# Five moving operands stored packed, each row at 192 bytes modulo 512

## The chip, the cores and the metric

The kernel runs on one core of one Trainium2 chip. The metric is the device time of one execution in microseconds (us). The kernel before takes 1623.28 us, the median of three runs (1623.12 to 1624.36). A difference of 0.2% (3.2 us) is about what a measurement of this kernel can tell from none.

## What is computed

The reference is one layer of a decoder over 272 tokens (16 meta tokens and 256 real ones) with 2048 channels: a mixer of two branches (forgetting attention and gated linear attention) and an MLP with a squared ReLU. Cut to the parts that matter here:

```python
proj = xn @ w_in                                   # 2048 -> 13336, all branches' inputs
o_fox = forgetting_attention(fq, fk, fv, ff, b_forget)
o_gla = head_rmsnorm(gated_linear_attention(gq, gk, gv, g_log)) * silu(gr)
y = sigmoid(gate_fox) * (o_fox @ w_o_fox) + sigmoid(gate_gla) * (o_gla @ w_o_gla)
h = h + y @ w_out
h = h + square(relu(rmsnorm(h) @ w1)) @ w2         # 2048 -> 8192 -> 2048
return rmsnorm(h)[:, 16:]
```

All inputs and weights are float32, and some 290 MB of weights are read once.

## The kernel before, in words

Channels lie on the 128 partitions and tokens on the free axis. A product takes one block of 128 output columns of a weight matrix: 16 row tiles (KT = 16) of 128 by 128 weights against the 16 row tiles of an activation, summed in one PSUM bank.

float32 accuracy comes from splitting each factor in two float32r parts. `next_weights` (L125) takes the next block off the list that `stream` (L40) lays out, as two halves of 8 row tiles: SP issues the load of `raw` (L118), ACT rounds it to `whi` (L120), DVE makes the rest `wlo` (L121). The pool holds five halves of each, so loads and splits run ahead of the products until a buffer is missing. The activation is split the same way by `split_to` (L168) or by a pair like L793 and L794, into an upper and a lower part that lie in one tile.

`gemm2` (L139) is the product that the change touches. For each of its row tiles it calls `mac2` (L135), which issues two matmuls: `whi` times upper and lower part at once, 512 columns wide (L136), and `wlo` times the upper part, 256 columns (L137). Each matmul is preceded by a load of its 128 columns of weights into the array (LDWEIGHTS). This text calls the two matmuls of one row tile, the wide and the narrow one, **a pair**. So 16 pairs make a product of 2048 inputs, and 8 pairs one of the forgetting branch's outputs, which have 1024.

The moving operands of `gemm2`, in the order of their use:

| operand | what it is | pairs | row step, bytes | lower part behind the upper, bytes | first row modulo 512 | row starts modulo 512 |
|---|---|---|---|---|---|---|
| `x` (L231) | normalised input | 928 | 2176 | 1088 | 128 | 128, 256, 384, 0 in turn |
| `of` (L633) | output of forgetting attention | 128 | 2048 | 1024 | 128 | all at 128 |
| `og` (L434) | output of linear attention | 256 | 2112 | 1056 | 64 | 64, 128, 192, ... in turn |
| `y` (L752) | gated sum | 256 | 2176 | 1024 | 128 | 128, 256, 384, 0 in turn |
| `x2` (L760) | input of the MLP | 1024 | 2112 | 1024 | 64 | 64, 128, 192, ... in turn |
| `a` (L822, four tiles) | hidden layer, a quarter each | 960 | 2176 | 1088 | 64 | 64, 192, 320, 448 in turn |

Where the lower part is 1024 bytes behind the upper one, the 512 columns of L136 are one unbroken run; else they are two runs with a gap between. The addresses are those of the built program. The rows of weights are 512 bytes each, and all of them start at 128 modulo 512. `a` is also read by the products of the last four output blocks, outside `gemm2`: narrow ones at L848, and L864 with 128 columns of each part.

`operand` (L221) makes the tiles of `og`, `y`, `x2` and `a`, with a step per row and an offset; `of` is a plain tile. Tiles with the tag "s1" (`x`, `y`, `a`) share one place, and so do those with the tag "s2" (`room`, `og`, `x2`, `whi_last`), as wide as its widest tile, 33,792 bytes a partition. `room` is scratch of the first half of the kernel.

Order of the work: four heads of linear attention and eight of forgetting attention, all on `x`; then 8 rounds of two output blocks, with gate products on `x`, then `of`, then `og`; then 16 products on `y`; then four times 16 products on `x2` and 16 on `a`. Within an engine a scheduler orders the instructions at build time.

Of the kernel before, what the change touches and what calls it, by code (L numbers as in the profile page):

```python
# [7 lines left out]
F32 = mybir.dt.float32  # L8
F32R = mybir.dt.float32r
# [7 lines left out]
P = 128  # L17
D = 2048
KT = D // P
NM = 16  # L20
NT = 256
NA = NM + NT
EPS = 1e-6
FOX_H, FOX_D = 8, 128
# [41 lines left out]
def trunk(ctx: ExitStack, tc: tile.TileContext, hT, w_small, w_all, consts, w_alpha2, out):  # L66
# [3 lines left out]
    def nm(s):  # L70
        serial[0] += 1
        return f"{s}_{serial[0]}"

    const = ctx.enter_context(tc.tile_pool(name="const", bufs=1))
    keep = ctx.enter_context(tc.tile_pool(name="keep", bufs=1))
# [49 lines left out]
    def next_weights(keep_hi=None):  # L125
        c = chunk[0]
        chunk[0] += 1
        parts = []
        for i in range(2):
            hi, lo, step = weight_half(c, i, None if keep_hi is None else keep_hi[:, HK * i : HK * (i + 1), :])  # L130
            step(0, HK)
            parts.append((hi, lo))
        return lambda k: (parts[k // HK][0][:, k % HK, :], parts[k // HK][1][:, k % HK, :])
# [5 lines left out]
    def gemm2(w, x, k0=0, nk=KT):  # L139

        ps = bank(pg, "ps")
        for k in range(nk):
            hi, lo = w(k0 + k)
            mac2(ps, hi, lo, x[:, k], k == 0, k == nk - 1)
        issued()
        return ps
# [12 lines left out]
    def total(ps, t=None):  # L159

        b = tmp.tile([P, NT], F32, tag="evb", name=nm("evb"))
        nc.scalar.copy(b, ps[:, NT:512])  # L162
        if t is None:
            t = tmp.tile([P, NT], F32, tag="evt", name=nm("evt"), bufs=4)
        nc.vector.tensor_tensor(t, ps[:, 0:NT], b, op=ALU.add)  # L165
        return t
# [51 lines left out]
            done = t + P  # L218
        nc.tensor.matmul(ps[:, 0:n], ones[:, 0:P], d, start=True, stop=True)

    def operand(pool, name, per_k, per_half, at=0, tag=None):  # L221


        kw = {} if tag is None else {"tag": tag}
        t = pool.tile([P, KT, per_k], F32R, name=nm(name), **kw)
        return t[:, :, at : at + per_half + NT].rearrange("p k (o t) -> p k o t", t=NT) if per_half == NT else \
            t[:, :, at : at + 2 * per_half].rearrange("p k (o t) -> p k o t", t=per_half)[:, :, :, 0:NT]


    h = keep.tile([P, KT, NA + 3], F32, name="h")  # L230
# [2 lines left out]
    ident, scan = cons[:, 0:P], cons[:, P : P + NA]  # L233
    ggn, ba, bf = cons[:, 400:416], cons[:, 416:424], cons[:, 424:425]

    room = keep.tile([P, KT * 2 * NT], F32, tag="s2", name="room")
    at_room = [0]

    def take(*shape):
# [13 lines left out]
    def gain(i, k):  # L253
        return h[:, k, NA + i : NA + i + 1]
# [57 lines left out]
    for s in range(KT // 2):  # L312
# [5 lines left out]
        for kk in range(2):  # L318
            k = 2 * s + kk
# [8 lines left out]
        at = [(w[0][:, c], w[1][:, c]) for w, n in ((wa, 4), (wb, 3)) for c in range(n)]  # L328
# [101 lines left out]
    og_box = []  # L430

    def og_tile():
        if not og_box:
            og_box.append(operand(keep, "og", 528, 264, tag="s2"))  # L434
        return og_box[0]

    def gla_gates(ts):
# [20 lines left out]
    def gla_head(hd, sg, ready=None):  # L458
# [122 lines left out]
        def scale():  # L581
            pr = st["pr"]
            spread(pr, st["y"], (0, P), NT)
            nc.scalar.copy(rg, pr[:, 0:NT])
            for i in range(4):
                j = 4 * hd + i
                nc.vector.scalar_tensor_tensor(oT[:, i, :], oT[:, i, :], ggn[:, j : j + 1], rg, op0=ALU.mult,
                                               op1=ALU.mult)
                nc.vector.tensor_tensor(oT[:, i, :], oT[:, i, :], st["sg"][:, i, :], op=ALU.mult)
                split_to(og_tile()[:, j, 0, :], og_tile()[:, j, 1, :], oT[:, i, :])  # L590
# [34 lines left out]
    for hd in range(1, GLA_H):  # L625
        gla_head(hd, None)
    flush()
    og = og_tile()


    cum.close()
    late = ctx.enter_context(tc.tile_pool(name="late", bufs=1, reuse_waits="tile"))
    of = late.tile([P, FOX_H, 2, NT], F32R, name="of")  # L633
    negc = late.tile([P, FOX_H, NA], F32, name="negc")
    nc.gpsimd.dma_start(negc.rearrange("p h t -> p (h t)"), fdram.to_broadcast([P, FOX_H * NA]))
    fox = ExitStack()
# [105 lines left out]
    for j0 in range(0, KT, 2):  # L742
        gates = ahead if j0 == 0 else [gate() for _ in range(4)]
        w = next_weights()
        for j in range(2):
            t = total(gemm2(w, of, k0=8 * j, nk=8))
            nc.vector.tensor_tensor(gates[2 * j], gates[2 * j], t, op=ALU.mult)
        for j in range(2):
            t = total(gemm2(next_weights(), og))
            nc.vector.tensor_tensor(t, gates[2 * j + 1], t, op=ALU.mult)  # L750
            nc.vector.tensor_tensor(yf[:, j0 + j, :], gates[2 * j], t, op=ALU.add)
    y = operand(keep, "y", 544, NT, at=16, tag="s1")  # L752
    for j in range(KT):
        split_to(y[:, j, 0, :], y[:, j, 1, :], yf[:, j, :])
    mix.close()
# [1 line left out]


    ht = h[:, :, NM:NA]
    x2 = operand(keep, "x2", 528, NT, tag="s2")  # L760

    def square_sum(j, acc):
        if j == 0:
            nc.scalar.activation(acc, ht[:, j, :], AF.Square)
        else:
            sq = gat.tile([P, NT], F32, tag="hsq", name=nm("hsq"))
            nc.scalar.activation(sq, ht[:, j, :], AF.Square)  # L767
            nc.gpsimd.tensor_tensor(acc, acc, sq, op=ALU.add)  # L768

    def add_residual(j, ps):  # L770
        b = tmp.tile([P, NT], F32, tag="evb", name=nm("evb"))
        nc.scalar.copy(b, ps[:, NT:512])
        nc.vector.tensor_tensor(ht[:, j, :], ps[:, 0:NT], ht[:, j, :], op=ALU.add)
        nc.vector.tensor_tensor(ht[:, j, :], ht[:, j, :], b, op=ALU.add)
# [38 lines left out]
    def relu2(a, f, ps):  # L813
        t = total(ps)
        nc.vector.scalar_tensor_tensor(t, t, 0.0, r2b, op0=ALU.max, op1=ALU.mult)
        s = gat.tile([P, NT], F32, tag="asq", name=nm("asq"))
        nc.vector.tensor_tensor(s, t, t, op=ALU.mult)
        split_to(a[:, f, 0, :], a[:, f, 1, :], s)

    acc = gat.tile([P, NT], F32, tag="acc", name="acc3", bufs=1)  # L820
    for g in range(NG):
        a = operand(keep, "a", 544, 272, tag="s1")  # L822
        held = []
        for f in range(KT):
            ps = gemm2(next_weights(), x2)
            if g == 0 and f == 0:
                held.append(ps)
                continue
            if g == 0 and f == 1:
                relu2(a, 0, held.pop())  # L830
            relu2(a, f, ps)
        last = g == NG - 1
        for j in range(KT - NL if last else KT):
            add_residual(j, gemm2(next_weights(), a))
            if last:
                square_sum(j, acc)
                nc.scalar.activation(ht[:, j, :], ht[:, j, :], AF.Identity, scale=gain(2, j))
                if j == 0:
                    tc.keep_in_program_order(nc.scalar.preload_act_table_set("sqrt_and_others"))
# [55 lines left out]
    v, p, none = nc.vector, nc.gpsimd, lambda: None  # L895
# [81 lines left out]
```

## Time and profile before

| | us |
|---|---|
| median of three runs | 1623.28 |
| the profiled execution | 1623.76 |
| its span, first to last instruction | 1621.7 |
| TensorE busy with matmuls (PE) | 1609.0 |
| weight loads (PEld) | 1447.0 |
| VectorE (DVE) | 1030.6 |
| ScalarE (ACT) | 787.8 |
| GpSimd (POOL) | 92.8 |

A row of the profile's groups names the line of the kernel, the engine, the operation, the tiles written and read, shapes and a count, then the busy time and the mean duration of one in ns, then the idle time before. Buffer numbers are left out of tile names, so that `x2` shows as `x`; the two are told apart by time, since `x` is last read at 786 us and `x2` first at 892 us. Matmuls overlap in the pipeline: the end of one, and so its duration, is modelled and reaches past the next one's start. The time that a matmul costs is the distance from its start to the next start. The view in order of time gives starts to 0.01 us.

### The profile page before, as it was taken

How to read it: one execution, taken by the hardware profiler on the slowest of the kernel's cores; microseconds unless marked ns; L12 is line 12 of the kernel's file. 1: busy time of each engine (PE TensorE's matmuls, PEld its weight loads, DVE VectorE, ACT ScalarE, POOL GpSimd, SP SyncE). 2: the span in 40 equal slices, each digit the busy share in tenths (PEclk: the TensorE clock that was granted, in tenths of full speed). 3: DMA queues.
4: the chain of work that ended last, by engine and by line, in shares of the span. 5: the costliest groups of instructions: out<-in, count | busy, mean ns of one | idle time of the engine just before them, and what ended most of it. 6: DMA issues, size and time to landing. Idle time of an engine off the chain costs nothing.

```text
span 1621.7 us, 25628 instructions
## 1 busy us (share of the span) xinstructions
PE 1609.0 (99%) x10000; PEld 1447.0 (89%) x10000; DVE 1030.6 (64%) x1589; ACT 787.8 (49%) x1212; POOL 92.8 (6%) x144
## 2 busy tenths in 40 slices
PE   9999999999999999999999999999999999999997
PEld 8999999999998888888888888888888888888887
DVE  7866747476555555555677766567655676567654
ACT  6655444454445444444555444444444444444553
POOL 1000000010000000000011000000000000000022
PEclk9999999999999999999999999999999999999998
DMA  9444445454445555555555555555565555555552
GB/s 315 149 142 159 163 158 170 155 197 158 156 157 174 189 186 191 185 191 185 190 188 192 183 189 188 190 187 189 181 195 188 190 187 189 188 189 188 187 180 89
DMA packets 90841, 292.96 MB, mean 181 GB/s; under 512 B 9160, under 2 KB 21712, under 8 KB 90592
## 3 DMA queue, kind: packets, MB, share of 16 engines
q1 hardware_dynamic: 89472, 289.69, 55.1%
q8 instruction: 78, 1.28, 0.3%
q0 software_dynamic: 176, 1.12, 0.2%
q10 hardware_dynamic: 1072, 0.52, 0.1%
q14 instruction: 43, 0.35, 0.1%
HBM read 289.19 MB, written 2.11 MB: 180 GB/s over the span
## 4 chain that ended last, share of the span: by engine, by line
PE 99%; DMA 0%; ACT 0%; DVE 0%; SPq 0%; issue 0%; DVEq 0%; ACTq 0%
PE ps L136 51%; PE ps L137 26%; PE psa L155 5%; PE psa L154 5%; PE psa L153 5%; PE ps L334 1%; PE ps L864 1%; PE ps L339 1%; PE pa L504 1%; PE ps L848 0%; DMA h<-hT_dram 0%; PE po L568 0%; PE pz L402 0%; PE po L569 0%; PE pq L665 0%; PE po L182 0%
## 5 line engine op out<-in xcount | busy, mean ns | idle before, releaser
L121 DVE TENSOR_TENSOR wlo<-raw,whi 128x1024 fp32r<-128x1024 f32 x522 | 639.7, 1225 | 497.4 <-ACT whi L120 496.1
L120 ACT CAST whi<-raw 128x1024 fp32r<-128x1024 f32 x522 | 548.3, 1050 | 744.1 <-PE ps L136 502.0
L136 PE MATMUL ps<-x,whi 128*128 128x512 f32 x1952 | 685.8, 394 | 0.0
L137 PE MATMUL ps<-x,wlo 128*128 128x256 f32 x1952 | 548.0, 281 | 0.0
L136 PEld LDWEIGHTS ps<-x,whi 128*128 128x128 f32 x1952 | 366.4, 188 | 83.2
L137 PEld LDWEIGHTS ps<-x,wlo 128*128 128x128 f32 x1952 | 367.1, 188 | 0.0
L136 PE MATMUL ps<-a,whi 128*128 128x512 f32 x960 | 335.8, 394 | 0.0
L137 PE MATMUL ps<-a,wlo 128*128 128x256 f32 x960 | 269.7, 282 | 0.0
L136 PEld LDWEIGHTS ps<-a,whi 128*128 128x128 f32 x960 | 180.1, 188 | 41.0
L153 PE MATMUL psa<-x,whi 128*128 128x272 f32 x640 | 186.3, 291 | 0.0
L155 PE MATMUL psa<-x,whi 128*128 128x272 f32 x640 | 186.0, 291 | 0.0
L154 PE MATMUL psa<-x,wlo 128*128 128x272 f32 x640 | 184.5, 288 | 0.0
L137 PEld LDWEIGHTS ps<-a,wlo 128*128 128x128 f32 x960 | 181.4, 189 | 0.4
L153 PEld LDWEIGHTS psa<-x,whi 128*128 128x128 f32 x640 | 121.1, 189 | 0.7
L154 PEld LDWEIGHTS psa<-x,wlo 128*128 128x128 f32 x640 | 120.4, 188 | 0.2
L155 PEld LDWEIGHTS psa<-x,whi 128*128 128x128 f32 x640 | 120.2, 188 | 0.1
L136 PE MATMUL ps<-og,whi 128*128 128x512 f32 x256 | 89.9, 393 | 0.0
L136 PE MATMUL ps<-y,whi 128*128 128x512 f32 x256 | 89.1, 392 | 0.0
L768 POOL TENSOR_TENSOR acc<-acc,hsq 128x256 f32<-128x256 f32 x26 | 28.8, 1110 | 774.4 <-ACT hsq L767 774.4
L137 PE MATMUL ps<-y,wlo 128*128 128x256 f32 x256 | 71.8, 281 | 0.0
L137 PE MATMUL ps<-og,wlo 128*128 128x256 f32 x256 | 71.7, 280 | 0.0
L165 DVE TENSOR_TENSOR evt<-ps,evb 128x256 f32<-128x256 f32 x158 | 65.8, 417 | 0.2 <-ACT evb L162 0.2
(263 smaller groups left out, 1384.7 us busy)
## 6 DMA issues: line engine op xcount, KB each, us to landing
raw<-w_all_dram SPq DMA_DIRECT2D x537, 512.0 KB, 4.0
raw<-w_all_dram SPq DMA_DIRECT2D x7, 384.0 KB, 6.0
h<-hT_dram SPq DMA_DIRECT2D x7, 275.0 KB, 6.1
out_dram<-h SPq DMA_DIRECT2D x5, 256.0 KB, 2.6
negc<-fdram POOLq DMA_DIRECT2D x1, 1088.0 KB, 6.1
raw<-w_all_dram SPq DMA_DIRECT2D x2, 256.0 KB, 3.7
raw<-w_all_dram SPq DMA_DIRECT2D x2, 192.0 KB, 3.8
room<-w_small_dram SPq DMA_DIRECT2D x1, 320.0 KB, 6.9
```

The lines of the kernel that those rows point to most:

```text
L120: nc.scalar.copy(hi[:, k, :], r)
L121: nc.vector.tensor_tensor(lo[:, k, :], r, hi[:, k, :].bitcast(F32), op=ALU.subtract)
L136: nc.tensor.matmul(ps, hi, x, start=first, stop=False)
L137: nc.tensor.matmul(ps[:, 0:NT], lo, x[:, 0, :], start=False, stop=last)
L153: nc.tensor.matmul(ps[:, 0:n], hi, x[:, k, 0, :], start=(k == 0), stop=False)
L154: nc.tensor.matmul(ps[:, 0:n], lo, x[:, k, 0, :], start=False, stop=False)
L155: nc.tensor.matmul(ps[:, 0:n], hi, x[:, k, 1, :], start=False, stop=(k == KT - 1))
L165: nc.vector.tensor_tensor(t, ps[:, 0:NT], b, op=ALU.add)
L334: nc.tensor.matmul(ps, hi, x[:, k, :, NM:NA], start=st, stop=False)
L339: nc.tensor.matmul(ps[:, 0:NT], lo, x[:, k, 0, NM:NA], start=False, stop=sp)
L504: nc.tensor.matmul(dst, k[:, a, :], q[:, a, :], start=(a == 0), stop=(a == 1))
L768: nc.gpsimd.tensor_tensor(acc, acc, sq, op=ALU.add)
```

## The change

`operand` makes all five tiles `of`, `og`, `y`, `x2` and `a`. Rows are 2048 bytes, upper and lower part side by side, and `at` floats ahead of the first row place it: 32 floats (128 bytes) in the tiles that start at 64 modulo 512, and 16 floats (64 bytes) in `of`, whose tile starts at 128. So each row of the five starts at 192 modulo 512. `room` is made as wide as `og` was, which keeps the place of "s2" at 33,792 bytes and the tiles of weights where they were, at 128 modulo 512. `x` is as before. The tiles of the pool of `of` that lie behind it move by 64 bytes.

```diff
-    def operand(pool, name, per_k, per_half, at=0, tag=None):
-        kw = {} if tag is None else {"tag": tag}
-        t = pool.tile([P, KT, per_k], F32R, name=nm(name), **kw)
-        return t[:, :, at : at + per_half + NT].rearrange("p k (o t) -> p k o t", t=NT) if per_half == NT else \
-            t[:, :, at : at + 2 * per_half].rearrange("p k (o t) -> p k o t", t=per_half)[:, :, :, 0:NT]
+    def operand(pool, name, at, nk=KT, **kw):
+        t = pool.tile([P, at + nk * 2 * NT], F32R, name=nm(name), **kw)
+        return t[:, at:].rearrange("p (k o t) -> p k o t", o=2, t=NT)
...
-    room = keep.tile([P, KT * 2 * NT], F32, tag="s2", name="room")
+    room = keep.tile([P, 264 * 2 * KT], F32, tag="s2", name="room")
...
-            og_box.append(operand(keep, "og", 528, 264, tag="s2"))
+            og_box.append(operand(keep, "og", 32, tag="s2"))
...
-    of = late.tile([P, FOX_H, 2, NT], F32R, name="of")
+    of = operand(late, "of", 16, FOX_H)
...
-    y = operand(keep, "y", 544, NT, at=16, tag="s1")
+    y = operand(keep, "y", 32, tag="s1")
...
-    x2 = operand(keep, "x2", 528, NT, tag="s2")
+    x2 = operand(keep, "x2", 32, tag="s2")
...
-        a = operand(keep, "a", 544, 272, tag="s1")
+        a = operand(keep, "a", 32, tag="s1")
```

In the built programs the instructions of every engine stand in the same order and number; on all of them only one wait differs, a copy on GpSimd (L655) that no longer waits for DVE.

## The prediction, as put on record before the run

> **What bounds the kernel now.** I read the page's busy times first, then the chain that ended last, then the clock.
>
> ```profile
> PE 1609.0 (99%) x10000; PEld 1447.0 (89%) x10000; DVE 1030.6 (64%) x1589; ACT 787.8 (49%) x1212; POOL 92.8 (6%) x144
> ```
> ```profile
> PE 99%; DMA 0%; ACT 0%; DVE 0%; SPq 0%; issue 0%; DVEq 0%; ACTq 0%
> PE ps L136 51%; PE ps L137 26%; PE psa L155 5%; PE psa L154 5%; PE psa L153 5%; PE ps L334 1%; PE ps L864 1%; PE ps L339 1%; PE pa L504 1%; PE ps L848 0%; DMA h<-hT_dram 0%; PE po L568 0%; PE pz L402 0%; PE po L569 0%; PE pq L665 0%; PE po L182 0%
> ```
> ```profile
> core 0: 1621.7 us, clock 0.997
> ```
>
> TensorE sets the end from first to last: 99% of the chain, and L136 with L137, the pairs of `gemm2`, are 77% of it. The granted clock is 0.997, so there is no throttle to win back. A nanosecond per pair counts one to one, as long as nothing else takes over. How many pairs there are, from the groups (`x` holds 928 pairs of `x` itself and 1024 of `x2`):
>
> ```profile
> L136 PE MATMUL ps<-x,whi 128*128 128x512 f32 x1952 | 685.8, 394 | 0.0
> ...
> L136 PE MATMUL ps<-a,whi 128*128 128x512 f32 x960 | 335.8, 394 | 0.0
> ...
> L136 PE MATMUL ps<-og,whi 128*128 128x512 f32 x256 | 89.9, 393 | 0.0
> L136 PE MATMUL ps<-y,whi 128*128 128x512 f32 x256 | 89.1, 392 | 0.0
> ```
>
> With 128 pairs of `of` (below), 960 + 1024 + 256 + 256 + 128 = 2624 pairs read an operand that the change moves. What a pair costs I take from the view in order of time, from the first wide matmul of a stage to the first of the next:
>
> ```profile
> 511.50 0.39 PE L136 MATMUL ps<-of,whi 128*128 128x512 f32 x1
> ...
> 517.15 0.40 PE L136 MATMUL ps<-og,whi 128*128 128x512 f32 x1
> ...
> 528.35 0.39 PE L136 MATMUL ps<-x,whi 128*128 128x512 f32 x1
> ...
> 802.94 0.39 PE L136 MATMUL ps<-y,whi 128*128 128x512 f32 x1
> ...
> 892.11 0.39 PE L136 MATMUL ps<-x,whi 128*128 128x512 f32 x1
> ...
> 1071.93 0.40 PE L136 MATMUL ps<-x,whi 128*128 128x512 f32 x1
> ...
> 1161.31 0.39 PE L136 MATMUL ps<-a,whi 128*128 128x512 f32 x1
> ...
> 1250.90 0.40 PE L136 MATMUL ps<-x,whi 128*128 128x512 f32 x1
> ```
>
> - `of`: 16 pairs in 517.15 - 511.50 = 5.65 us, 353.1 ns each
> - `og`: 32 pairs in 528.35 - 517.15 = 11.20 us, 350.0 ns
> - `y`: 256 pairs in 892.11 - 802.94 = 89.17 us, 348.3 ns
> - `x2`: 256 pairs in 1161.31 - 1071.93 = 89.38 us, 349.1 ns
> - `a`: 256 pairs in 1250.90 - 1161.31 = 89.59 us, 350.0 ns
>
> All pairs together: 960 x 350.0 + 1024 x 349.1 + 256 x 348.3 + 256 x 350.0 + 128 x 353.1 ns = 336.0 + 357.5 + 89.2 + 89.6 + 45.2 = 917.5 us, a mean of 349.6 ns. The same work differs by 5 ns a pair with the layout alone. Inside one product of `x2` the spread is larger; these are wide matmuls of four rows in turn (starts at 64, 128, 192 and 256 modulo 512):
>
> ```profile
> 1099.86 0.39 PE L136 MATMUL ps<-x,whi 128*128 128x512 f32 x1
> ...
> 1100.21 0.40 PE L136 MATMUL ps<-x,whi 128*128 128x512 f32 x1
> ...
> 1100.57 0.39 PE L136 MATMUL ps<-x,whi 128*128 128x512 f32 x1
> ...
> 1100.91 0.40 PE L136 MATMUL ps<-x,whi 128*128 128x512 f32 x1
> ```
>
> The row is found by counting: 1100.57 lies 28.64 us behind 1071.93, which is 5 products of 5.586 us and 2.03 pairs, so it is the third row. The row at 128 takes 0.36 us to the next pair, that at 192 takes 0.34, that at 64 takes 0.35. The groups in two windows of 0.04 us, which hold one wide matmul each, say it in ns, first the row at 128 and then that at 192:
>
> ```profile
> L136 PE MATMUL ps<-x,whi 128*128 128x512 f32 x1 | 0.4, 397 | 0.0
> ```
> ```profile
> L136 PE MATMUL ps<-x,whi 128*128 128x512 f32 x1 | 0.4, 387 | 0.0
> ```
>
> So 10 ns of 512 columns hang on where the row starts against the weights, whose rows all start at 128.
>
> **The change part by part.** No instruction is added, removed or moved; the terms are the cost of a pair and what stands around it.
>
> Term 1, the start. Each of the 2624 pairs now starts at 192. The nearest row of the trace is the packed `x2` row at 192, 0.34 us: the same start, the same unbroken 512 columns, the same weights. It has one difference: its neighbours start at 128 and 256, and in the changed kernel they start at 192 too. That neighbours matter is shown at the start 128, which three packed layouts have. `x2` takes 0.36 us there (above). In `y`, where the next row is at 256, the row at 128 is the pair that starts at 850.31:
>
> ```profile
> 850.31 0.39 PE L136 MATMUL ps<-y,whi 128*128 128x512 f32 x1
> ...
> 850.65 0.39 PE L136 MATMUL ps<-y,whi 128*128 128x512 f32 x1
> ```
>
> 0.34 us. And `of` starts at 128 in every row, which is the form that the change gives to all five:
>
> ```profile
> 511.85 0.40 PE L136 MATMUL ps<-of,whi 128*128 128x512 f32 x1
> ...
> 512.21 0.40 PE L136 MATMUL ps<-of,whi 128*128 128x512 f32 x1
> ...
> 512.56 0.40 PE L136 MATMUL ps<-of,whi 128*128 128x512 f32 x1
> ...
> 512.91 0.40 PE L136 MATMUL ps<-of,whi 128*128 128x512 f32 x1
> ```
> ```profile
> L136 PE MATMUL ps<-of,whi x128: 387/398/403, 511.5 to 791.4; 128*128 128x512 f32 x128
> ```
>
> 0.36, 0.35, 0.35: not even equal rows cost the same, the wide matmul lasts 387 at the least, 398 in the median and 403 at the most. So a start has a tendency, and the neighbours add or take some 6 ns. The ends for the new pair are the row at 192 and `of`, the only constant start. The first is 0.34 us in the view; finer, its wide matmul lasts 387 ns and the mean of that stage is 393:
>
> ```profile
> L136 PE MATMUL ps<-x,whi 128*128 128x512 f32 x256 | 89.4, 393 | 0.0
> ```
>
> 349.1 - 6 = 343, and I put it at 344 ns. The second is 353.1 ns. I take **346 ns**: nearest to the row that shares the start, with a third of the way back to the mean of 349.6, because its neighbours go. Sum: 2624 x 346 ns = 907.9 us, against 917.5 us: **9.6 us less**.
>
> Term 2, the unbroken run. `og` and `a` had their 512 columns in two runs and cost 350.0, `y` and `x2` in one and cost 348.3 and 349.1. That 1 to 2 ns is inside term 1, since 346 is for packed rows; it speaks for the packing apart from the start.
>
> Term 3, the last blocks. `a` is read by 64 and 128 more narrow matmuls:
>
> ```profile
> L864 PE MATMUL ps<-a,whi_last 128*128 128x256 f32 x128 | 16.2, 282 | 0.0
> ...
> L848 PE MATMUL ps<-a,wlo 128*128 128x256 f32 x64 | 8.0, 279 | 0.0
> ```
>
> Their means are 3 ns apart. At 4 ns each either way, 192 of them are worth 0.8 us at most. I take nothing.
>
> Term 4, what writes the operands. ACT and DVE write the same 256 columns, in unbroken runs as before. Both have room:
>
> ```profile
> 1072.00:1161.20 89.20, 89.20 (x513) 78.23 (x513) 62.74 (x94) 42.49 (x63) 0.00 (x0) 1.00 0.59 189
> ```
> ```profile
> ACT whi L120 <- PE ps L136: 502.0, 340, 3.8
> ```
>
> In this stage of `x2`, PE fills 89.20 of 89.20 us, DVE 62.74 and ACT 42.49, and the DMA share is 0.59. ACT waits 502 us for PE to give a weight buffer back: the weights are ahead, not behind. With PE 1% faster that cover shrinks by about 1 us per stage of 26, so nothing else becomes late. Without that cover a microsecond of DVE would cost a microsecond; here it costs nothing. The wait that GpSimd loses at L655 frees an engine that is busy 6% of the span, at no gain.
>
> Sum against the profiled execution: 1623.76 - 9.6 = 1614.2 us. That execution was 0.5 us over the median of the runs, so against the median: 1623.28 - 9.6 = **1613.7 us**.
>
> [...]
>
> **The rivals.**
>
> *Constant starts lock into a slow order (slower).* Place: every pair of the five operands. Mechanism: with all rows alike, nothing averages the stall between weight load and moving read; the pairs fall into one repeated pattern, as those of `of` do. For it: `of` is the only constant layout and is the slowest of the five. Against it: it stands at 128, where `x2` is slowest too, and 192 is where `x2` is fastest. Price: 2624 x 353.1 = 926.5 us, 9.0 us more, 1632.3 us. It decides from a pair above 349.6 ns on; to be told from no change it needs 351.
>
> *The mean stays (no change).* Rows only lend each other time: the row at 192 is short because the one at 128 before it was long (0.36 and 0.34 make 0.70, which is twice 0.35), and the cyclic layouts lie within 348.3 to 350.0. Then a pair stays at about 349.6: 1623.3 us. Against it: `of` at 353.1 shows that a mean can leave that band. [...]
>
> *The change does less than it says* (the rows do not all reach 192, or the weights move): not so in the built program; no chance of its own.
>
> **How the numbers follow.** Forecast, pairs of 342.5 to 348.3 ns (1605 to 1620 us): 0.62. Mean stays, within 0.2% (about what a measurement of this kernel can tell from no change; 348.4 to 350.9 ns): 0.13. Slow order, above 1626.5 us: 0.25, most of it up to the 353.1 ns of `of`. The forecast's own range is 1605 to 1620; to leave out no more than 2 in 10 the range goes on to the price of the slow order: 1605 to 1632.5. So faster 0.62, same 0.13, slower 0.25.
>
> **What would show it.** In the view in order of time, the stages of `x2` and `a` give pairs near 346 ns, 88.6 us for 256, against 89.38 and 89.59, and all five operands agree within 1 ns, since they now have one layout. The wide matmul's mean falls from 392 to 398 towards 389. A mean of 397 or more, or a wide spread in `x2`, shows the slow order. Stages of unequal cost would make the reading by start address wrong: then something else, such as the buffers of weights, sets the stall. The pairs on `x` and the L153 to L155 products must not move.

## The result, and the profile after

The changed kernel takes 1629.29 us (median of six runs, 1628.55 to 1629.66) against 1623.34 us of the kernel before (six runs): a ratio of 1.0035, with a 95% interval of 1.0022 to 1.0048. It is slower by some 6 us where 9.6 us less was forecast. The profiled execution has a span of 1626.7 us, 5.0 us more than before, at the same granted clock:

```profile
core 0: 1626.7 us, clock 0.998
```

The page's busy times, and two groups of pairs from it, in the same columns as before:

```profile
PE 1613.9 (99%) x10000; PEld 1448.1 (89%) x10000; DVE 1031.0 (63%) x1589; ACT 787.5 (48%) x1212; POOL 92.2 (6%) x144
...
L136 PE MATMUL ps<-x,whi 128*128 128x512 f32 x1952 | 688.2, 395 | 0.0
...
L136 PE MATMUL ps<-a,whi 128*128 128x512 f32 x960 | 337.8, 395 | 0.0
```

PE carries the difference alone (1609.0 to 1613.9 us); DVE, ACT and the counts stand still, and the groups of pairs show no idle time, before or after. The wide matmuls last 395 ns where 394 was before. That mean hides what happened. The first wide matmul of each stage, from the view in order of time (`x2` shows as `x`):

```profile
802.59 0.39 PE L136 MATMUL ps<-y,whi 128*128 128x512 f32 x1
...
892.93 0.40 PE L136 MATMUL ps<-x,whi 128*128 128x512 f32 x1
...
983.37 0.39 PE L136 MATMUL ps<-a,whi 128*128 128x512 f32 x1
...
1073.71 0.40 PE L136 MATMUL ps<-x,whi 128*128 128x512 f32 x1
...
1164.17 0.39 PE L136 MATMUL ps<-a,whi 128*128 128x512 f32 x1
...
1254.61 0.39 PE L136 MATMUL ps<-x,whi 128*128 128x512 f32 x1
...
1345.06 0.40 PE L136 MATMUL ps<-a,whi 128*128 128x512 f32 x1
...
1434.50 0.39 PE L136 MATMUL ps<-x,whi 128*128 128x512 f32 x1
...
1523.81 0.40 PE L136 MATMUL ps<-a,whi 128*128 128x512 f32 x1
```

Each stage has 256 pairs. `y` takes 90.34 us, 352.9 ns a pair (348.3 before). The second `x2` takes 90.46 us, 353.4 ns, the third 90.45 us, 353.3, but the fourth 89.31 us, 348.9 (349.1 before). The second `a` takes 90.44 us, 353.3, the third 89.44 us, 349.4 (350.0 before). **One layout, one line, one operand, and two costs.** Ahead of these stages `of` and `og` have them too: 353 ns in the first of their eight rounds and 349 in the other seven; in the kernel before `of` had 353 in all eight. Added up over the trace, `y` costs 1.2 us more than before, `x2` 2.3 and `a` 2.0, and `of` 0.4 less.

The groups of two windows say it of `x2` in ns, first in its second stage (1075 to 1164 us) and then in its fourth (1436 to 1523 us):

```profile
L136 PE MATMUL ps<-x,whi 128*128 128x512 f32 x253 | 89.4, 396 | 0.0
```
```profile
L136 PE MATMUL ps<-x,whi 128*128 128x512 f32 x250 | 87.3, 393 | 0.0
```

Inside these stages the view in order of time shows the wide matmuls repeating. In the second stage (slow):

```profile
1119.65 0.39 PE L136 MATMUL ps<-x,whi 128*128 128x512 f32 x1
...
1119.99 0.40 PE L136 MATMUL ps<-x,whi 128*128 128x512 f32 x1
...
1120.35 0.40 PE L136 MATMUL ps<-x,whi 128*128 128x512 f32 x1
...
1120.71 0.39 PE L136 MATMUL ps<-x,whi 128*128 128x512 f32 x1
```

0.34, 0.36 and 0.36 us, 1.06 us for three pairs, and so on through the stage. In the fourth:

```profile
1480.20 0.39 PE L136 MATMUL ps<-x,whi 128*128 128x512 f32 x1
...
1480.55 0.39 PE L136 MATMUL ps<-x,whi 128*128 128x512 f32 x1
...
1480.90 0.40 PE L136 MATMUL ps<-x,whi 128*128 128x512 f32 x1
...
1481.25 0.39 PE L136 MATMUL ps<-x,whi 128*128 128x512 f32 x1
```

0.35 us each, 1.05 us for three. I call such a repetition an **order**. All rows here start at 192, so neither the start nor the neighbours' starts can tell one stage from the other. (The page's means, 396 and 393 ns, are modelled durations; the distances of the starts are the cost.)

### The profile page after: what moved, and what is told of

It reads as the page before. It is cut to its first block, busy times and chain, and to the rows that moved or that the text cites. A ratio compares the mean times of both kernels' runs of the same rounds, so it can differ in the third digit from the quotient of the medians.

```text
span 1626.7 us, 25627 instructions
## 1 busy us (share of the span) xinstructions
PE 1613.9 (99%) x10000; PEld 1448.1 (89%) x10000; DVE 1031.0 (63%) x1589; ACT 787.5 (48%) x1212; POOL 92.2 (6%) x144
## 4 chain that ended last, share of the span: by engine, by line
PE 99%; DMA 0%; ACT 0%; DVE 0%; SPq 0%; issue 0%; DVEq 0%; ACTq 0%
PE ps L136 51%; PE ps L137 26%; PE psa L155 5%; PE psa L154 5%; PE psa L153 5%; PE ps L331 1%; PE ps L861 1%; PE ps L336 1%; PE pa L501 1%; PE ps L845 0%; DMA h<-hT_dram 0%; PE po L565 0%; PE pz L399 0%; PE po L566 0%; PE pq L662 0%; PE po L182 0%
## 5 line engine op out<-in xcount | busy, mean ns | idle before, releaser
L153 PE MATMUL psa<-x,whi 128*128 128x272 f32 x640 | 186.3, 291 | 0.0
L155 PE MATMUL psa<-x,whi 128*128 128x272 f32 x640 | 186.0, 291 | 0.0
L153 PEld LDWEIGHTS psa<-x,whi 128*128 128x128 f32 x640 | 121.1, 189 | 0.7
L155 PEld LDWEIGHTS psa<-x,whi 128*128 128x128 f32 x640 | 120.2, 188 | 0.1
```

What stands on the lines that cost most here:

```text
L153: nc.tensor.matmul(ps[:, 0:n], hi, x[:, k, 0, :], start=(k == 0), stop=False)
L155: nc.tensor.matmul(ps[:, 0:n], hi, x[:, k, 1, :], start=False, stop=(k == KT - 1))
```

## The experiments

The leading theory (order theory): the stall of a matmul depends on where its reads stand against the weight load beside it and on the state that the pairs before left. With equal starts the state repeats itself, and what came before a stage picks one of a few orders. Its rivals: the start theory (each start has its own cost), and the packing theory (the unbroken run of 512 columns is the loss).

Pair costs in this section are worked out from the first wide matmul of one product to that of the eighth product behind it, which is 128 pairs. The stretch starts at the third product of `y`, the fifth of the first `x2` and of `a`, and the seventh of the other `x2`; the last `a` has 12 products, so there it is 7 products, or 112 pairs. The middle of a stage shows its order without the disturbed first products (see e6). The fences of the experiments show such starts, from the view in order of time of the kernel that the section is about; the columns are the start in us, the modelled duration in us, engine, line, operation, tiles and shape. The costs in ns a pair, in the order of the stages:

| kernel | y | x2 | a | x2 | a | x2 | a | x2 | a | time, us |
|---|---|---|---|---|---|---|---|---|---|---|
| changed, all at 192 | 353.3 | 348.9 | 353.3 | 353.3 | 353.3 | 353.3 | 348.9 | 348.9 | 353.4 | 1629.29 |
| e1, other constant starts | 353.3 | 346.7 | 353.3 | 353.3 | 346.7 | 346.7 | 351.1 | 353.3 | 353.3 | 1628.89 |
| e2, stepping starts | 349.2 | 349.2 | 350.0 | 349.2 | 349.2 | 349.2 | 350.0 | 349.2 | 350.0 | 1622.96 |
| e3, parts apart, 192 | 351.1 | 351.1 | 351.1 | 351.1 | 351.1 | 351.1 | 351.1 | 351.1 | 351.1 | 1627.36 |
| e4, weights step, 192 | 350.8 | 350.8 | 350.8 | 350.8 | 350.8 | 350.8 | 350.8 | 350.8 | 350.8 | 1626.05 |
| e5, 128 and 384 | 346.7 | 346.7 | 346.7 | 346.7 | 353.4 | 353.4 | 346.7 | 346.7 | 353.4 | 1623.01 |
| e6, one swap a stage | 353.3 | 353.3 | 348.9 | 353.4 | 353.4 | 353.4 | 353.4 | 353.4 | 353.4 | 1630.06 |
| e8, same distance | 348.9 | 353.4 | 348.9 | 348.9 | 353.4 | 353.4 | 348.9 | 348.9 | 353.4 | 1627.66 |
| e11, x2 steps again | 353.3 | 349.2 | 353.3 | 349.2 | 348.9 | 349.2 | 348.9 | 349.2 | 348.9 | 1624.82 |
| e9, before, wides first | 346.9 | 350.0 | 349.2 | 350.0 | 349.2 | 350.0 | 349.2 | 350.0 | 349.2 | 1623.18 |
| e10, changed, wides first | 344.6 | 344.6 | 344.6 | 344.6 | 344.6 | 344.6 | 344.6 | 344.6 | 344.6 | 1610.55 |
| e12, wides first, other starts | 344.6 | 349.2 | 346.7 | 349.2 | 349.2 | 349.2 | 351.3 | 349.2 | 346.7 | 1621.81 |

e5, e9 and e10 are medians of several runs, the other experiments single runs beside the kernel before, which took 1623.44 to 1623.50 us there. The pair costs of a row are those of one profiled execution.

**e1: other constant starts.**

```diff
-            og_box.append(operand(keep, "og", 32, tag="s2"))
+            og_box.append(operand(keep, "og", 112, tag="s2"))
...
-    y = operand(keep, "y", 32, tag="s1")
+    y = operand(keep, "y", 96, tag="s1")
...
-    x2 = operand(keep, "x2", 32, tag="s2")
+    x2 = operand(keep, "x2", 80, tag="s2")
...
-        a = operand(keep, "a", 32, tag="s1")
+        a = operand(keep, "a", (0, 16, 48, 64)[g], tag="s1")
```

> The five operands packed as in the changed kernel, each still with one start for all its rows, but other starts: a at 64, 128, 256 and 320 modulo 512 in its four tiles, x2 at 384, y at 448, og at 0; of stays at 192. Order theory (equal starts let the pairs fall into one of a few repeated orders, and what came before picks the order): each stage repeats an order of a few pairs, some stages near 349 ns a pair and some near 353, with no start that is clean throughout, and x2, which has one start in four stages, may differ between them by 4 ns. Start theory (192 is a bad start among equals, others are good or bad by themselves): each start has one cost, the same in every stage of that start (x2: four stages within 0.5 ns), and the starts differ by up to 10 ns, 128 near the 353 that of had before.

The second and the third stage of `x2`, both at 384, 8 products each:

```profile
1108.23 0.40 PE L136 MATMUL ps<-x,whi 128*128 128x512 f32 x1
...
1153.45 0.40 PE L136 MATMUL ps<-x,whi 128*128 128x512 f32 x1
...
1286.98 0.39 PE L136 MATMUL ps<-x,whi 128*128 128x512 f32 x1
...
1331.35 0.39 PE L136 MATMUL ps<-x,whi 128*128 128x512 f32 x1
```

45.22 us against 44.37 us, 353.3 and 346.7 ns a pair at the same start: the start theory falls. The last three `x2` stages go by the `a` before them: behind `a` at 128 in 346.7 ns `x2` runs at 346.7, behind `a` in 353.3 or 351.1 at 353.3. The first does not: behind `y` in 353.3 it settles at 346.7, after matmuls of the norm (L208, L219) have stood among the pairs of its second and fourth product. The order theory's numbers were not right either: besides 353.3 there were 346.7 and 351.1, and not 349.

**e2: starts that step.** Each row's 512 columns are one unbroken run, but the rows are 2112 or 2176 bytes apart, and those of `a` are taken in a turned sequence, so that its starts step by 192, 320, 448 and 128 in the four tiles. The others step by 64, and `of` stays at 192.

```diff
+    def operand(pool, name, at, nk=KT, step=512, s=1, **kw):
...
-    x2 = operand(keep, "x2", 32, tag="s2")
+    x2 = operand(keep, "x2", 0, step=528, tag="s2")
...
-        a = operand(keep, "a", 32, tag="s1")
+        a = operand(keep, "a", 0, step=(528, 528, 528, 544)[g], s=(3, 5, 7, 1)[g], tag="s1")
...
+            return self.ap[(i[0], self.s * i[1] % KT, *i[2:])]
```

> All operands packed, but the starts step through the classes again: a by 192, 320, 448 and 128 modulo 512 from row to row in its four tiles, x2, y and og by 64 (x2 as in the kernel before); of stays constant at 192. Order theory: with stepping starts an order cannot repeat every few pairs, so every stage has one steady cost and lies within 348 to 350.5 ns, no stage jumps between two costs, and the four stages of x2 are back at 349.1. Start theory: each row costs what its start costs, so all steps that visit all eight starts (64, 192, 320, 448) have the same mean, 349.1, to 0.5 ns. Packing theory (the unbroken run of 512 columns is the loss): a, packed here, is above 350.0 in all its tiles, and x2 and y are unchanged.

Every stage is steady, and all four of `x2` are at 349.2. `a` is at 350.0 where its rows step by 192, 448 and 128, and at 349.2 by 320; stepping through the same eight starts does not give one mean, so the start alone is again not it. The packing theory falls too: packed with a step of 128, `a` costs the 350.0 that it cost with two runs before.

**e3: constant starts, the parts apart.**

```diff
-        t = pool.tile([P, at + nk * 2 * NT], F32R, name=nm(name), **kw)
-        return t[:, at:].rearrange("p (k o t) -> p k o t", o=2, t=NT)
+        gap = 16
+        t = pool.tile([P, at + nk * 2 * NT + gap], F32R, name=nm(name), **kw)
+        n = nk * NT + gap
+        return bass.AP(t.tensor, t.offset + at, [t.ap[0], [NT, nk], [n, 2], [1, NT]])
```

> The constant start of 192 as in the changed kernel, but the lower parts of all rows lie in a block of their own behind the upper parts, 64 bytes off modulo 512, so that the 512 columns are two runs, as a had before. Order theory and start theory: the slow cost stays, 352 to 354 ns a pair in most stages of a and x2, and the run is about as slow as the changed kernel, 1626 to 1632 us. Packing theory: the cost goes back to the 350 that a had, 1623 to 1624 us.

351.1 in every stage, 1627.36 us: between the two expectations, and neither met. All nine stages have one cost here, so the second run, or its start 64 bytes off, changes which orders there are; the two are not told apart. It is slower than `a` was before with two runs, so the packing is not the loss.

**e4: the weights step.** The operands stay, the rows of `wlo` are 544 bytes apart.

```diff
-        lo = wp.tile([P, HK, P], F32R, tag="wlo", name=nm("wlo"))
+        lo = wp.tile([P, HK, 136], F32R, tag="wlo", name=nm("wlo"))[:, :, 0:P]
...
-    room = keep.tile([P, 264 * 2 * KT], F32, tag="s2", name="room")
+    room = keep.tile([P, 260 * 2 * KT], F32, tag="s2", name="room")
```

> The changed kernel, with the rows of wlo 544 bytes apart in place of 512, so that the start of the narrow matmul's weights steps by 32 modulo 512 from row to row while the moving operands keep their constant start of 192 (of is at 448 here, since its tile moves). Theory that the stall lies between the weight load and the moving read: what counts is the distance between the two starts, so stepping the weights undoes the constancy as stepping the operand does, the repeated three pairs vanish, and a and x2 go to 348 to 350.5 ns, 1618 to 1624 us; pairs on x change a little too. Theory that the moving read stalls by its own address (its start alone): nothing changes, 353 ns in the slow stages, 1629 us.

The second stage of `x2`:

```profile
1106.07 0.39 PE L136 MATMUL ps<-x,whi 128*128 128x512 f32 x1
...
1150.98 0.39 PE L136 MATMUL ps<-x,whi 128*128 128x512 f32 x1
```

44.91 us, 350.8 ns, and the same in all nine stages: with the weights' rows stepping under the same operands the two orders are gone. That the moving read stalls by its own address falls. The size was off: 350.8 is over the 350.5 that I allowed, and 1626.05 us over 1624.

**e8: both moved, the distance kept.**

```diff
-    room = keep.tile([P, 264 * 2 * KT], F32, tag="s2", name="room")
+    room = keep.tile([P, 264 * 2 * KT + 16], F32, tag="s2", name="room")
...
-        a = operand(keep, "a", 32, tag="s1")
+        a = operand(keep, "a", 48, tag="s1")
```

The same 48 stands for `og`, `y` and `x2`.

> The changed kernel with the tiles of weights and the five operands both moved on by 64 bytes: operands start at 256 modulo 512, weights at 192, still 64 apart; x stays, so its distance to the weights changes. If the distance between weight load and moving read decides, the five operands keep the two orders of the changed kernel, 348.9 and 353.3 ns, and nothing else appears, while x leaves its 350.0. If the operand's own start decides, they take the 351.2 that a had at 256 with the weights at 128, and x stays at 350.0.

The first and the second stage of `x2`:

```profile
916.57 0.40 PE L136 MATMUL ps<-x,whi 128*128 128x512 f32 x1
...
961.80 0.39 PE L136 MATMUL ps<-x,whi 128*128 128x512 f32 x1
...
1107.34 0.39 PE L136 MATMUL ps<-x,whi 128*128 128x512 f32 x1
...
1151.99 0.39 PE L136 MATMUL ps<-x,whi 128*128 128x512 f32 x1
```

353.4 and 348.8 ns: the two orders of the changed kernel, and the 351.1 of the start 256 nowhere. So for constant starts the distance between the two starts decides which orders there are. One miss: `x` stayed at 350.0, though its distance had changed, so the distance is not yet an account of rows that step.

**e6: one swap a stage.**

```diff
+        if swap:
+            nc.tensor.matmul(ps[:, 0:NT], lo, x[:, 0, :], start=False, stop=False)
+            nc.tensor.matmul(ps, hi, x, start=False, stop=last)
+            return
...
-            mac2(ps, hi, lo, x[:, k], k == 0, k == nk - 1)
+            mac2(ps, hi, lo, x[:, k], k == 0, k == nk - 1, k == swap)
...
-            ps = gemm2(next_weights(), x2)
+            ps = gemm2(next_weights(), x2, swap=8 if f == 2 else None)
```

The same for the third product of `a`.

> The changed kernel; in the third product of each stage of x2 and of a, the narrow matmul of the ninth row is issued ahead of the wide one, 8 swaps in all, with the same sums. Order theory: a swap breaks the repetition, and behind it the pairs may settle in another order than before it: at least one stage changes between 353.3 and 348.9 ns at that product or differs from the changed kernel's stage, and no other cost than these two appears for long. Start theory: a swap costs or gains some 10 ns at its own place, and every stage goes on as in the changed kernel.

The starts of the first, third, fifth and ninth product of the second `x2` stage; the swap is in the third (wide matmuls are L140 here):

```profile
1073.20 0.40 PE L140 MATMUL ps<-x,whi 128*128 128x512 f32 x1
...
1084.36 0.39 PE L140 MATMUL ps<-x,whi 128*128 128x512 f32 x1
...
1095.64 0.40 PE L140 MATMUL ps<-x,whi 128*128 128x512 f32 x1
...
1118.25 0.39 PE L140 MATMUL ps<-x,whi 128*128 128x512 f32 x1
```

Ahead of the swap 11.16 us for 32 pairs, 348.8 ns; behind it 22.61 us for 64, 353.3, and that to the end of the stage. In the first `a` the pairs go from 353 ns ahead of the swap to 348.9 behind it. One exchange of two matmuls changes the cost of some 200 pairs behind it: a state is carried, and it picks the order. Not each swap does it: the third and the fourth stage of `x2` stand at 353.4 on both sides.

The kernels have such places without e6. In `y`, in the first `x2` and in each `a` the built program breaks the turn of wide and narrow once, in the second product, where two wide matmuls follow each other and then two narrow ones (in the first `x2` with matmuls of the norm between); in the third `a` of the changed kernel:

```profile
1353.90 0.63 PE L136 MATMUL ps<-a,whi 128*128 128x512 f32 x2
1354.37 0.40 PE L137 MATMUL ps<-a,wlo 128*128 128x256 f32 x2
```

Ahead of it the pairs cost the 353.3 ns in which the `x2` before had ended, behind it 348.9. In the changed kernel, e5 and e8 every stage behind `y` starts in the order in which the one before ended, in all 24 cases, and the orders change only at these breaks and at the norm's matmuls in the first `x2`. The other three `x2` stages have no break and keep one order from end to end.

**e11: one part undone.** `x2` steps by 64 again, by the `operand` of e2; the rest stays at 192.

```diff
-    x2 = operand(keep, "x2", 32, tag="s2")
+    x2 = operand(keep, "x2", 0, step=528, tag="s2")
```

> The changed kernel with one part undone: x2 has its starts stepping by 64 modulo 512 again, as before; of, og, y and a stay at 192. Order theory: x2 is back at 349.1 ns a pair in all four stages and leaves the same state behind each time, so the second, third and fourth stage of a, which follow the same thing, settle in the same order as each other, all 348.9 or all 353.3 ns (with the changed kernel they were 353.3, 348.9 and 353.3). Start theory: a is at one cost in all its stages in both kernels.

The second and the third stage of `a`:

```profile
1185.07 0.39 PE L136 MATMUL ps<-a,whi 128*128 128x512 f32 x1
...
1229.72 0.39 PE L136 MATMUL ps<-a,whi 128*128 128x512 f32 x1
...
1363.86 0.39 PE L136 MATMUL ps<-a,whi 128*128 128x512 f32 x1
...
1408.52 0.39 PE L136 MATMUL ps<-a,whi 128*128 128x512 f32 x1
```

44.65 and 44.66 us, 348.8 and 348.9 ns, and the fourth `a` at 348.9 as well: the same order three times, as the order theory has it. `a` itself is as in the changed kernel, where its second and fourth stage were at 353.3 and 353.4. But the first `a` stands at 353.3, though the `x2` before it costs 349.2 like the others. The rows of that `x2` tell it apart. The first four rows of the seventh product (starts at 64, 128, 192 and 256), in the first stage of `x2` and then in the second:

```profile
927.07 0.39 PE L136 MATMUL ps<-x,whi 128*128 128x512 f32 x1
...
927.42 0.40 PE L136 MATMUL ps<-x,whi 128*128 128x512 f32 x1
...
927.78 0.39 PE L136 MATMUL ps<-x,whi 128*128 128x512 f32 x1
...
928.12 0.40 PE L136 MATMUL ps<-x,whi 128*128 128x512 f32 x1
```
```profile
1106.78 0.39 PE L136 MATMUL ps<-x,whi 128*128 128x512 f32 x1
...
1107.12 0.39 PE L136 MATMUL ps<-x,whi 128*128 128x512 f32 x1
...
1107.47 0.39 PE L136 MATMUL ps<-x,whi 128*128 128x512 f32 x1
...
1107.82 0.39 PE L136 MATMUL ps<-x,whi 128*128 128x512 f32 x1
```

0.35, 0.36 and 0.34 us against 0.34, 0.35 and 0.35. In the mean of the stretch the row at 64 takes 354 ns in the first stage and 345 in the other three, and the row at 320 the other way round: the same eight costs, moved on by four rows. So even rows that step have more than one order, here with one mean, and the first `a` follows another state than the other three.

**e5: the starts that had shown 346.7.**

```diff
-    x2 = operand(keep, "x2", 32, tag="s2")
+    x2 = operand(keep, "x2", 80, tag="s2")
...
-        a = operand(keep, "a", 32, tag="s1")
+        a = operand(keep, "a", 16, tag="s1")
...
```

`y` is at 128 too, `og` at 384 and `of` at 128.

> Constant starts again, packed, but those at which a stage of 346.7 ns a pair was seen (a at 128 modulo 512, x2 at 384, two stages of four), for all: a, y and of at 128, x2 and og at 384. Order theory: the orders of these two starts are 346.7 and about 353.3 ns, nothing in between, and which one a stage has depends on the one before it; with 346.7 once reached and kept, a and x2 give 1984 x 2.9 ns = 5.8 us less than the kernel before, 1615 to 1619 us; if the stages fall into 353.3, 1629 to 1632 us. Start theory: a start has one cost, so a is at 346.7 in all four stages, and x2 cannot be at 346.7 in one stage and 353 in another.

As the order theory has it, the table shows two orders, 346.7 and 353.4, and nothing between them; the time fell between both forecasts, 1623.01 us, a ratio of 0.9998 (0.9988 to 1.0007), since six of the nine stages took the one and three the other. With wide and narrow by turns, choosing these starts does not give the good order, because the start does not choose the order.

**e7, e10: wide matmuls first.** The changed layout, with another sequence in `gemm2`.

```diff
-        for k in range(nk):
-            hi, lo = w(k0 + k)
-            mac2(ps, hi, lo, x[:, k], k == 0, k == nk - 1)
+        for k in range(0, nk, HK):
+            for i in range(k, k + HK):
+                nc.tensor.matmul(ps, w(k0 + i)[0], x[:, i], start=i == 0, stop=False)
+            for i in range(k, k + HK):
+                nc.tensor.matmul(ps[:, 0:NT], w(k0 + i)[1], x[:, i, 0, :], start=False, stop=i == nk - 1)
```

> The changed kernel with another sequence in every product of gemm2: 8 wide matmuls, then the 8 narrow ones of the same rows, in place of wide and narrow by turns. If each matmul's stall comes from the weight load that runs beside it alone, the sums stay: wides about 231 ns and narrows about 118, within 348 to 354 a pair, 1622 to 1631 us. If the stall comes from a wide and a narrow following each other (the jump back in the operand), the wides fall towards the least seen, 225 ns, and the total by over 10 us.

1610.83 us: the second reading, though the wides did not reach 225 (228.7 ns from start to start, the mean of the 840 in `a` that a wide follows). Whether the jump back in the operand or the change of width costs the time in the turn of wide and narrow is not told apart. The same kernel, over several runs:

> The changed layout with 8 wide and then 8 narrow matmuls, as seen once at 1610.83 us, now timed against the kernel before: 1609.5 to 1612 us, a ratio of 0.992, in every run, since no stage has more than one order.

1610.55 us against 1623.50 us, a ratio of 0.9922 (0.9907 to 0.9937). It beats both kernels. The second stage of `x2` in e10:

```profile
1098.74 0.39 PE L144 MATMUL ps<-x,whi 128*128 128x512 f32 x1
...
1142.84 0.39 PE L144 MATMUL ps<-x,whi 128*128 128x512 f32 x1
```

44.10 us, 344.5 ns by these rounded starts, and 344.6 in all nine stages of the table: at this start the sequence shows one order only.

**e9: the sequence without the layout.** The same edit in the kernel before.

> The kernel before, with its own layouts, and the sequence of 8 wide and then 8 narrow matmuls in gemm2. If the sequence alone gave the 344.6 ns a pair, the layouts do not matter under it: all five operands are at 344 to 345.5 and the time is 1609 to 1612 us. If the equal starts at 192 were needed, the pairs stay near the 350 of the kernel before, at least those of a, og and x2, and the time is 1619 to 1624 us.

1623.18 us, a ratio of 0.9998 (0.9989 to 1.0008): `x2` at 350.0 and `a` at 349.2, so the sequence gives nothing without the equal starts. The layout gives its gain only with the sequence, and the sequence only with the layout. (The 346.9 of `y` holds one product of its disturbed beginning; behind it `y` runs at 346.7.)

**e12: wides first, other starts.** The edits of e1 and of e7 together.

> 8 wide and then 8 narrow matmuls, with the constant starts of the second kernel of this study: a at 64, 128, 256 and 320 modulo 512, x2 at 384, y at 448, og at 0, of at 192. Under this sequence each start gives one cost, the same in all four stages of x2; the costs of the starts spread by 2 to 8 ns a pair around 344.6. If a start below 343 is there, that start for all would be under 1607 us; if all lie within 1 ns of 344.6, the sequence sets the cost and the start nothing.

The second stage of `x2` (384), and the third of `a` (256):

```profile
1104.18 0.40 PE L144 MATMUL ps<-x,whi 128*128 128x512 f32 x1
...
1148.87 0.40 PE L144 MATMUL ps<-x,whi 128*128 128x512 f32 x1
...
1361.24 0.40 PE L144 MATMUL ps<-a,whi 128*128 128x512 f32 x1
...
1406.20 0.40 PE L144 MATMUL ps<-a,whi 128*128 128x512 f32 x1
```

44.69 us, 349.1 ns, and 44.96 us, 351.3 ns. Here each start has one cost, `x2` the same in all four stages, and starts 256 apart agree: 64 and 320 give 346.7, 128 and 384 give 349.2, 192 and 448 give 344.6. With wides first 192 and 448 are the best of the starts tried; none is below 343. In this sequence the start theory holds for constant starts. It does not hold for rows that step: in e9 `y`, which steps through 128, 256, 384 and 0, costs less (346.9) than 128, 256 and 384 do here.

## Why the prediction was wrong

- **What bounds the kernel**: right. PE sets the end before and after, and the groups of pairs never wait for DVE or ACT. The pairs on `x` stayed at 350 ns and L153 to L155 as they were. Terms 2, 3 and 4 gave or cost nothing that can be seen: the narrow matmuls of the last blocks last 283 and 280 ns where they had 282 and 279, and e2 shows that the unbroken run is worth nothing for `a` at a step of 128.
- **Term 1 is the step that failed.** It put each of the 2624 pairs at 346 ns, nearest to the `x2` row at 192, and took a start to have a tendency that its neighbours bend by some 6 ns. The runs show in its place that in the sequence wide, narrow, wide, narrow a row has no cost of its own: with the same start and the same neighbours a pair of `x2` costs 348.9 or 353.3, by the order that the stage fell into (changed kernel, e6; in e1 346.7 or 353.3). The 344 of that row was one beat of an order of eight rows, with 349.1 as its mean. In e11, where `x2` lies as in the kernel before, the row at 192 takes 344 ns in one stage and 346 in three, and the row at 128 takes 358 and 348. The 10 ns between these two rows, read as the start's doing, were the place in the order.
- **The slow rival** named the mechanism, that equal rows lock into one repeated pattern, and its price, 353.1, was `of`'s and close to the 353.3 that came. Where it was wrong: not every pair goes there. Of the nine stages in the table six did, and three took 348.9; so the time is 1629.29 us and not 1632.3. `of` itself, whose cost was the price, took 349 in seven of its eight rounds. The sign that was set, a wide matmul of 397 ns or more, did not come even in a slow stage, which shows 396.
- **Its chance** was too low at 0.25. The one constant layout in the trace, `of`, spoke for it, and I set against it a row of a stepping layout, which is another case. The note in the prediction that unequal stages would refute the reading by start was the right test; it named the weights' buffers as the other cause. An order holds through many products, while the buffers, five halves of each, come round every two and a half; and e6 changes the order without touching them.
- **The mean stays**: not that either. With wide and narrow by turns the stepping layouts kept to 348.3 to 350.0 in the kernel before and in e2, constant ones run from 346.7 to 353.4.
- **What a page says of these reads**: the Trainium skill, "TensorE: Matmul & The Clock Gate", "Step-by-step: what each phase is for", says that TensorE has two independent read ports, and that loading the next weights takes no read bandwidth from the running matmul. By that alone, where the weights lie should not matter. In these runs it does: with the operands at 192 as they were, rows of weights that step took the slow pair from 353.3 to 350.8 (e4). The measurement decides; whether read bandwidth is what falls short, no run shows.

What stays open: why the distance between the two starts costs time, in the memory or in the array, and what the state is that lasts from pair to pair. That the place of the weights takes part is shown by e4 and e8; where the weight load meets the moving read was not measured. Each kernel with two orders has one trace, so whether a whole execution always falls into the same orders was not seen either. For it: the changed kernel, e6 and e11 are alike to the end of `y`, and all three took the same orders up to there; and the six times of the changed kernel lie within 1.1 us, which is what one stage in the other order would move (256 pairs at 4.4 ns).

## What to carry to other kernels

When one engine runs a long repeated sequence with nothing between, its cost per step can be a property of the repetition and not of the step: look whether one line has two costs in two stages before a price is taken from single rows, and price a constant layout by a constant layout. A layout and the sequence that reads it have to be tried together; here each alone was worth nothing or a loss, and both together 0.8%. Look also for the places where the built program breaks the sequence: they are where the cost can change.

## What the runs showed of the hardware that was not expected

- The cost of a pair came in steps: with constant starts of operands and weights, and wide and narrow by turns, the nine stages settled at 346.7, 348.9, 351.1 or some 353.3 ns, and at nothing between (e1, e3, e5, e8). A settled order lasts until the turn of wide and narrow is broken, over some 90 us and more, and it passes into the next stage (24 times of 24 in the changed kernel, e5 and e8). Two matmuls exchanged can switch it (e6).
- The starts of the weights' rows and of the operand's constant rows act through their distance: both moved by 64 bytes, the same two orders, 348.9 and 353.3 ns, were there (e8).
- With wides first and the weights at 128 modulo 512, a constant start has one cost, the same for starts 256 bytes apart, from 344.6 ns (192, 448) to 351.3 ns (256) (e10, e12).
